# Weight-stationary products: the 512-column and 256-column matmuls of a block grouped by width

## The chip, the cores and the metric

The kernel runs on one core of one Trainium2 chip. The metric is the device time in microseconds of one execution; a version's time is the median over its runs. The profile is one execution of the same program, recorded instruction by instruction.

## The reference

A decoder trunk of two residual layers on 256 tokens of width 1024, in float32, and a last RMSNorm. Every layer is half a SwiGLU feed-forward (inner width 2816), a token mixer, and half of a second feed-forward:

```python
def swiglu(h, w_gate, w_up, w_down):
    return (jax.nn.silu(h @ w_gate) * (h @ w_up)) @ w_down

for layer in range(DEPTH):
    x = x + 0.5 * swiglu(rmsnorm(x, norm_ffn1[layer]), ffn1_gate[layer], ffn1_up[layer], ffn1_down[layer])
    h = rmsnorm(x, norm_mix[layer])
    x = x + (even_mixer if layer % 2 == 0 else odd_mixer)(h, ...)
    x = x + 0.5 * swiglu(rmsnorm(x, norm_ffn2[layer]), ffn2_gate[layer], ffn2_up[layer], ffn2_down[layer])
return rmsnorm(x, norm_final)
```

The even mixer is stick-breaking attention (8 heads) beside a causal pooling, the odd mixer is block attention with 16 heads. Both begin with one projection of h (queries, keys, values) and end with one of the mixed result. So nearly all the arithmetic is products of a 256-row activation with large weight matrices.

## The kernel before

**Precision.** TensorE multiplies in float32r. To keep the accuracy, each operand is split in two parts, hi (rounded to float32r) and lo (the rest), and a product is the sum of three: hi·hi, hi·lo, lo·hi. Weights arrive from DRAM in units of 1 MB into `raw` tiles (L56, on SP's queue). ScalarE casts a unit to its hi part `whi` (L73) and VectorE subtracts to get the lo part `wlo` (L74), in two pieces of 1024 columns each. There are three raw buffers and four buffers each for `whi` and `wlo`; `ahead` keeps the split three units in front of their use.

**Three kinds of product.** `proj` (L336) keeps the activation in the array as the stationary operand and streams weight columns, 512 or 256 at a time. `rows` (L360) does that for the down projections and the output projections, always with 512 columns. `proj_W` (L399), the function that is changed, keeps the weights in the array: for one block of 128 output features it has 16 matmuls, two for each of the eight slices k of the model width. The first takes the hi weights of k and streams 512 columns: the 256 tokens of the hi part of the activation and, right behind them in the tile `xhl`, the 256 of its lo part. Its result covers a whole PSUM bank. The second takes the lo weights of k and streams only the 256 hi columns; its result is added to the second half of the same bank. Below, H is a matmul of 512 columns and L one of 256. Every matmul has its own weight load (PEld in the profile). `whole` then adds the two halves of the bank (ScalarE copy at L408, VectorE add at L409).

**Order of a block before.** H and L alternate with k: H0 L0 H1 L1 and so on to H6 L6, then L7 and H7, so that the first and the last matmul of the group cover the whole bank. The weights of a block come from two units of four slices each, or from one unit of eight.

**Where such blocks are.** Each of the four feed-forwards has five chunks of 512 features, each with four gate blocks and four up blocks: 40 blocks, 160 in all. The mixers' queries and keys are 8 blocks in the even layer and 16 in the odd (`qk_half`). That makes 184 blocks of 16 matmuls, 2944 in all.

**What sets the order of the work.** The program is written in order; a recording layer then places the instructions of each engine with its own estimates of durations, so that VectorE's and ScalarE's order between blocks comes from it. `Tasks` inserts small pieces of attention work (riders) between matmuls: `proj_W` calls `tasks.step()` after every eighth matmul. The PSUM accumulators come from a ring of five banks (`acc`), the small work from a ring of three (`tr`).

Of the kernel before, what the change touches and what calls it, by code (L numbers as in the profile page):

```python
# [13 lines left out]
PSUM = bass.MemoryType.PSUM  # L14
# [14 lines left out]


class WeightStream:
    """Weights from DRAM in 1 MB units, each split exactly into a float32r part and a rest."""

    def __init__(self, nc, pool, raw_bufs, split_bufs, load_ahead, split_ahead):
        self.nc, self.pool = nc, pool
# [22 lines left out]
            self.loaded += 1  # L58

    def split_piece(self):  # L60
        """The next piece of the next unit."""
        i = self.split
        if i not in self.parts:
            self.load_to(i + 1)
            self.now = [
                self.pool.tile([P, 2048], F32R, tag=f"w{x}", name=f"w{x}{i}", bufs=self.split_bufs) for x in ("hi", "lo")
            ]
            self.parts[i] = tuple(t.rearrange("p (k f) -> p k f", k=self.src[i][1]) for t in self.now)
            self.at = 0
        hi, lo = self.now  # L70
        raw = self.raw[i]
        r = slice(self.at, self.at + 1024 // self.pieces(i))
        self.nc.scalar.copy(hi[:, r], raw[:, r])  # L73
        self.nc.vector.tensor_sub(lo[:, r], raw[:, r], hi[:, r].bitcast(F32))  # L74
        self.at = r.stop
        if r.stop == 2048:
            self.raw.pop(i)
            self.split += 1
# [13 lines left out]


class Tasks:
    """Work that rides along with the stream of matrix products, a few blocks after its source."""

    def __init__(self):
        self.now = 0
# [18 lines left out]
def trunk_kernel(  # L117
# [24 lines left out]
    mm = nc.tensor.matmul  # L142
    tasks = Tasks()

# [1 line left out]
    ws = WeightStream(nc, wp, raw_bufs=3, split_bufs=4, load_ahead=6, split_ahead=3)  # L146
    plan = {}

# [36 lines left out]
                add_rows(("odd", "o", r), odd_w_o[0], 2 * r)  # L185
        add_ffn(("f2", layer), ffn2_gate[layer], ffn2_up[layer], ffn2_down[layer])

# [1 line left out]
    x = [ap_.tile([P, D], F32, tag=f"x{m}", name=f"x{m}") for m in range(2)]  # L189
    gains = [tp.tile([P, 384], F32, tag="az", name=f"gains{j}", bufs=2) for j in range(2)]  # L190

# [12 lines left out]
    load_gain(1, 16, norm_ffn2)  # L204
    load_gain(1, 32, even_pool_scale)

# [1 line left out]
    nc.scalar.preload_act_table_set("silu_and_others")  # L208
    warm = cp.tile([P, 512], BF16, name="warm")
    nc.vector.memset(warm, 0.0)  # L210

    def warm_up(n):
        """Keeps the tensor engine busy, so that its clock is up, while it has no operands yet."""
        bank = tr_bank()
        for _ in range(n):
            nc.tensor.matmul(bank, warm[:, 0:P], warm, start=True, stop=True)
# [7 lines left out]
    nc.gpsimd.memset(ones, 1.0)  # L224
    neg1 = cp.tile([P, P], F32, name="neg1")
    nc.gpsimd.memset(neg1, -1.0)
    # ntri[s', s] = -1 where s' >= s
    ntri = cp.tile([P, P], F32, name="ntri")
    nc.gpsimd.affine_select(ntri, neg1, pattern=[[-1, P]], compare_op=ALU.is_ge, fill=0.0, base=0, channel_multiplier=1)
    # past[s, t] = 1 where s < t; cap[s, t] = BIG where s < t, else 0; each twice side by side  # L230
    past = cp.tile([P, 2, P], F32, name="past")
    cap = cp.tile([P, 2, P], F32, name="cap")
    nc.gpsimd.memset(past, 1.0)
# [15 lines left out]
            for key, j, c in (("f1", 0, 0), ("mix", 1, 0), ("f2", 1, 16)) for layer in range(2)}  # L249
    turn_gains(0)  # L250

    # bands[g]: (s, t) weights of the window mean minus the token itself; s 0-127 x t 0-255, s 128-255 x t 128-255
    bands = [cp.tile([P, 384], F32, name=f"band{g}") for g in range(4)]
    # dist[t, s] = t - s, BIG where s > t; t 0-127 x s 0-127, t 128-255 x s 0-255
    dist = cp.tile([P, 384], F32, name="dist")
    gfin = cp.tile([P, D], F32, name="gfin")
    wpool = cp.tile([P, 4, P], F32, name="wpool")
# [28 lines left out]

    tasks.add(24, late_constants)

# [1 line left out]
    xhl = ap_.tile([P, KD, 2, T], F32R, tag="xhl", name="xhl")  # L290
    xh, xl = xhl[:, :, 0, :], xhl[:, :, 1, :]

    def norm_half(m, key, st, between=lambda: None, pool_q=(), square_first=False):
        """xT (times the gain) of token tile m as hi and lo parts, and 1/rms per token."""
        sq = tp.tile([P, D], BF16, tag="sq", name=uid("sq"), bufs=1)
        ss = tp.tile([P, 1], F32, tag=f"ss{m}", name=uid("ss"))
        if square_first:
            nc.scalar.activation(sq, x[m], AF.Square, accum_out=ss)
        t = []
        for q in range(2):  # L300
            bank = tr_bank()
            for j in range(4):
                k = 4 * q + j
                nc.tensor.transpose(bank[:, j * P : (j + 1) * P], x[m][:, k * P : (k + 1) * P], ident)  # L304
            t.append(tp.tile([P, 4, P], F32, tag="h", name=uid("xg"), bufs=2))
            nc.vector.tensor_mul(t[q], bank.rearrange("p (k t) -> p k t", k=4),
                                 gcol[key][:, 4 * q : 4 * q + 4, None].to_broadcast([P, 4, P]))
        for q in range(2):
            dst = (slice(None), slice(4 * q, 4 * q + 4), slice(m * P, (m + 1) * P))
            nc.scalar.copy(xh[dst], t[q])  # L310
            (nc.gpsimd if q in pool_q else nc.vector).tensor_sub(xl[dst], t[q], xh[dst].bitcast(F32))
            between()
        if not square_first:
            nc.scalar.activation(sq, x[m], AF.Square, accum_out=ss)
        ms = tp.tile([P, 1], F32, tag=f"ms{m}", name=uid("ms"))
        nc.gpsimd.tensor_scalar(ms, ss, 1.0 / D, EPS, op0=ALU.mult, op1=ALU.add)
        rstd = tp.tile([P, 1], F32, tag=f"rstd{m}", name=uid("rstd"))
        st["last"] = nc.gpsimd.tensor_tensor(rstd, ms, half, op=ALU.pow).ins
        st[m] = rstd
# [2 lines left out]
        return ((lhs_hi, rhs_hi), (lhs_hi, rhs_lo), (lhs_lo, rhs_hi))  # L322

    def proj(units, m, width):
        """PSUM tile of xT(m)^T @ W for a chunk of columns."""
        bank = acc_bank()
        ms = slice(m * P, (m + 1) * P)
        seq = []
        k = 0
        for i in units:  # L330
            hi, lo = ws.get(i)
            for kk in range(hi.shape[1]):
                seq += passes(xh[:, k, ms], xl[:, k, ms], hi[:, kk, :width], lo[:, kk, :width])
                k += 1
        for n, (a, b) in enumerate(seq):
            mm(bank[:, :width], a, b, start=(n == 0), stop=(n == len(seq) - 1))  # L336
            if n % (3072 // width) == 3072 // width - 1:
                tasks.step()
        return bank

    def rows(acc, groups, ah, al, scale, after, ready=None):
        """x += scale[m] * a^T @ W with the rows of W streamed; after(m) when x of m is complete."""
        total = sum(len(g) for g in groups) * 2
        done = {(m, n): 0 for m in range(2) for n in range(2)}
        for gi, group in enumerate(groups):
# [23 lines left out]
                        after(m, n)  # L369

    def first_products(ug, uu):
        """The products of the first chunk, in the order in which their operands arrive."""
        key = ("f1", 0)
        st = states[key]
        with tc.manual_schedule():
            norm_half(0, key, st, ws.split_piece, (1,), True)
            warm_up(3)
            ws.split_to(1)
            g0 = proj(ug, 0, 256)
            ws.split_to(2)  # L380
            norm_half(1, key, st, pool_q=(0, 1))
            u0 = proj(uu, 0, 256)
            ws.split_to(4)
            g1 = proj(ug, 1, 256)
            u1 = proj(uu, 1, 256)
        return [(g0, u0), (g1, u1)]

    def proj_W(units, f):
        """W[:, f]^T @ xT for all tokens: its large part in the first half of a bank, the rest in the second."""
        bank = acc_bank()  # L390
        n = 0
        k = 0
        fs = slice(f * P, (f + 1) * P)
        for i in units:
            hi, lo = ws.get(i)
            for kk in range(hi.shape[1]):
                both = ((hi, bank, xhl[:, k].rearrange("p a t -> p (a t)")), (lo, bank[:, T:], xhl[:, k, 0, :]))
                for w, dst, rhs in both if k < KD - 1 else both[::-1]:
                    mm(dst, w[:, kk, fs], rhs, start=(n == 0), stop=(n == 2 * KD - 1))  # L399
                    n += 1  # L400
                    if n % 8 == 0:
                        tasks.step()
                k += 1
        return bank

    def whole(bank, tag, bufs):
# [5 lines left out]
    def ffn(tag, st, after):  # L412
# [9 lines left out]
            nc.scalar.copy(hh[dst], v)  # L422
            nc.vector.tensor_sub(hl[dst], v, hh[dst].bitcast(F32))

        # the first chunk goes by token tiles, as one of them is complete before the other
        ug, uu = plan[tag, "g", 0], plan[tag, "u", 0]
        banks = first_products(ug, uu) if ug[0] == 0 else None
        ws.ahead(uu[-1])
# [34 lines left out]
        rows(acc, groups, hh, hl, hs, after)  # L463

    def mixer_tiles(n_f):
        """oT hi and lo, qT, kT and two tiles for 512 columns of token-major data, in the places of hT."""
        o = ap_.tile([P, KF, T], F32R, tag="hth", name=uid("o"))
        qk = ap_.tile([P, KF, T], F32, tag="htl", name=uid("qk"))
        tok1 = tp.tile([P, 2, 512], F32, tag="tok1", name=uid("tok1"), bufs=1)
# [2 lines left out]
        return o[:, 0:8, :], o[:, 8:16, :], q, k, (tok0, tok1)  # L472

    def bcast_rstd(st):
        """1/rms of every token on all partitions: [P, T]."""
        bank = tr_bank()
        dg = tp.tile([P, T], F32, tag="hw", name=uid("diag"), bufs=3)
        for m in range(2):
# [11 lines left out]
            nc.vector.scalar_tensor_tensor(dst[:, f0 + j, :], t, scale, rb, op0=ALU.mult, op1=ALU.mult)  # L490

    def pair_out(f, a0, a1, v, fv, oh, ol):
        """oT of two heads from their weights on (s, t), side by side in the columns of the tensor engine."""
        bank = acc_bank()
        for s, cols, start in ((slice(0, T), slice(0, T), True), (slice(T, 384), slice(P, T), False)):
            for j, a in enumerate((a0, a1)):
# [156 lines left out]
        units = [(plan["odd", "o", r], 2 * r) for r in range(4)]  # L653
        rows(acc, [units[0:2], units[2:4]], oh, ol, (1.0, 1.0), after, ready)

# [1 line left out]
    states = {}  # L657
    part = {}

    def finish(m, n):  # L660
        """The final norm of token tile m, after its half n of the columns."""
        r = slice(n * 512, (n + 1) * 512)
        if not part:
            xg = ap_.tile([P, 2, 2 * D], F32, tag="xhl", name=uid("xg"))
# [65 lines left out]
```

## Time and profile before

| | |
|---|---|
| median of 3 runs | 971.42 us (970.12 to 971.45) |
| profiled execution, first to last instruction | 968.9 us |
| PE busy, matmuls | 958.1 us, 99% of the span |
| PEld busy, weight loads beside them | 814.7 us |
| VectorE, ScalarE, GpSimd busy | 642.9, 521.1, 47.0 us |
| from DRAM | 169.63 MB, 176 GB/s over the span |

The profiled execution's own time is known as its span, 968.9 us; the median of the runs is 2.5 us above it; the difference lies outside the recorded span or is scatter between executions. "L399" is line 399 of the kernel before. A row such as "PE MATMUL acc<-xhl,whi 128*128 128x512" is a matmul that writes a tile `acc` from the streamed `xhl` with the weights `whi`, 128 rows by 128 columns of the array, 512 columns streamed. The recorded duration of a matmul holds its way through the array, so neighbours overlap in the record; what a matmul costs in a stream is the distance from its start to the start of the next, called its pitch here.

### The profile page before, as it was taken

How to read it: one execution, taken by the hardware profiler on the slowest of the kernel's cores; microseconds unless marked ns; L12 is line 12 of the kernel's file. 1: busy time of each engine (PE TensorE's matmuls, PEld its weight loads, DVE VectorE, ACT ScalarE, POOL GpSimd, SP SyncE). 2: the span in 40 equal slices, each digit the busy share in tenths (PEclk: the TensorE clock that was granted, in tenths of full speed). 3: DMA queues.
4: the chain of work that ended last, by engine and by line, in shares of the span. 5: the costliest groups of instructions: out<-in, count | busy, mean ns of one | idle time of the engine just before them, and what ended most of it. 6: DMA issues, size and time to landing. Idle time of an engine off the chain costs nothing.

```text
span 968.9 us, 13444 instructions
## 1 busy us (share of the span) xinstructions
PE 958.1 (99%) x5284; PEld 814.7 (84%) x5284; DVE 642.9 (66%) x1019; ACT 521.1 (54%) x891; POOL 47.0 (5%) x94
## 2 busy tenths in 40 slices
PE   8999999999999999999999999999999999999997
PEld 7888888888889888888888888888888798888885
DVE  6877764577566777754677777347887567777533
ACT  6655553375555555543456655336666466655432
POOL 6700000000000000000000000000000010000000
PEclk9999999999999999999999999999999999999999
DMA  8655554563425555545555555555533455555521
GB/s 313 242 176 193 199 202 187 174 214 134 131 88 178 200 198 202 179 174 181 181 204 174 174 179 202 218 183 173 175 131 121 140 175 174 174 179 200 208 108 44
DMA packets 84312, 171.55 MB, mean 177 GB/s; under 512 B 2788, under 2 KB 25880, under 8 KB 84248
## 3 DMA queue, kind: packets, MB, share of 16 engines
q1 hardware_dynamic: 83960, 170.17, 50.8%
q8 instruction: 41, 0.67, 0.3%
q10 hardware_dynamic: 288, 0.52, 0.1%
q14 instruction: 23, 0.19, 0.1%
HBM read 169.63 MB, written 1.05 MB: 176 GB/s over the span
## 4 chain that ended last, share of the span: by engine, by line
PE 97%; DMA 1%; ACT 0%; DVE 0%; SPq 0%; issue 0%; POOLq 0%; POOL 0%; ACTq 0%
PE acc L399 53%; PE acc L360 29%; PE acc L336 9%; PE tr L304 1%; PE acc L498 1%; DMA x<-in_x_dram 1%; PE tr L605 1%; PE tr L629 1%; PE tr L536 0%; PE tr L520 0%; PE tr L481 0%; DVE wlo L74 0%; SPq L56 0%; PE tr L572 0%; ACT whi L73 0%; PE tr L538 0%
## 5 line engine op out<-in xcount | busy, mean ns | idle before, releaser
L399 PE MATMUL acc<-xhl,whi 128*128 128x512 f32 x1472 | 511.3, 399 | 0.0
L74 DVE TENSOR_TENSOR wlo<-raw,whi 128x1024 fp32r<-128x1024 f32 (+1 forms) x324 | 385.6, 1212 | 174.0 <-ACT whi L73 172.4
L73 ACT CAST whi<-raw 128x1024 fp32r<-128x1024 f32 (+1 forms) x324 | 322.2, 1038 | 168.6 <-PE acc L360 87.0
L399 PE MATMUL acc<-xhl,wlo 128*128 128x256 f32 x1472 | 383.4, 281 | 0.0
L399 PEld LDWEIGHTS acc<-xhl,whi 128*128 128x128 f32 x1472 | 265.4, 188 | 51.9 <-issue 1.7
L399 PEld LDWEIGHTS acc<-xhl,wlo 128*128 128x128 f32 x1472 | 278.0, 189 | 16.5
L360 PE MATMUL acc<-whi,htl 128*128 128x512 f32 x352 | 137.3, 390 | 0.0
L360 PE MATMUL acc<-whi,hth 128*128 128x512 f32 x352 | 137.2, 390 | 0.0
L360 PE MATMUL acc<-wlo,hth 128*128 128x512 f32 x352 | 137.0, 389 | 0.0
L336 PE MATMUL acc<-whi,xhl 128*128 128x256 f32 (+1 forms) x416 | 92.5, 312 | 0.6 <-ACT whi L73 0.6
L360 PEld LDWEIGHTS acc<-whi,htl 128*128 128x128 f32 x352 | 66.1, 188 | 13.7
L360 PEld LDWEIGHTS acc<-wlo,hth 128*128 128x128 f32 x352 | 66.1, 188 | 13.7
L360 PEld LDWEIGHTS acc<-whi,hth 128*128 128x128 f32 x352 | 66.1, 188 | 13.3
L408 ACT COPY hw<-acc 128x256 f32<-128x256 f32 x104 | 38.4, 370 | 67.9 <-PE acc L399 67.9
L336 PEld LDWEIGHTS acc<-whi,xhl 128*128 128x128 f32 x416 | 68.6, 190 | 5.7 <-ACT whi L73 1.1
L409 DVE TENSOR_TENSOR hw<-hw,acc 128x256 f32<-128x256 f32 x104 | 43.3, 417 | 33.6 <-ACT hw L408 33.6
L336 PE MATMUL acc<-wlo,xhl 128*128 128x256 f32 (+1 forms) x208 | 64.2, 309 | 1.1 <-DVE wlo L74 1.1
L409 DVE TENSOR_TENSOR sg<-sg,acc 128x256 f32<-128x256 f32 x80 | 33.3, 417 | 40.5 <-ACT sg L408 40.5
L408 ACT COPY sg<-acc 128x256 f32<-128x256 f32 x80 | 29.4, 368 | 45.3 <-PE acc L399 45.3
L458 ACT CAST hth<-hw 128x256 fp32r<-128x256 f32 x80 | 32.5, 406 | 35.2 <-DVE hw L456 35.2
L452 ACT ACTIVATE sg<-sg 128x256 f32<-128x256 f32 x80 | 31.8, 417 | 29.6 <-DVE sg L451 29.6
L360 PE MATMUL acc<-whi,o 128*128 128x512 f32 x128 | 43.6, 404 | 0.0
(121 smaller groups left out, 597.6 us busy)
## 6 DMA issues: line engine op xcount, KB each, us to landing
raw<-in_ffn_down_dram SPq DMA_DIRECT2D x44, 1024.0 KB, 4.9
raw<-in_ffn_gate_dram SPq DMA_DIRECT2D x43, 1024.0 KB, 4.9
raw<-in_ffn_up_dram SPq DMA_DIRECT2D x43, 1024.0 KB, 4.9
raw<-in_odd_w_qkv_dram SPq DMA_DIRECT2D x12, 1024.0 KB, 5.0
raw<-in_even_w_in_dram SPq DMA_DIRECT2D x8, 1024.0 KB, 5.7
raw<-in_even_w_out_dram SPq DMA_DIRECT2D x4, 1024.0 KB, 4.9
raw<-in_odd_w_o_dram SPq DMA_DIRECT2D x4, 1024.0 KB, 4.9
raw<-in_ffn_gate_dram SPq DMA_DIRECT2D x2, 512.0 KB, 6.1
```

The lines of the kernel that those rows point to most:

```text
L73: self.nc.scalar.copy(hi[:, r], raw[:, r])
L74: self.nc.vector.tensor_sub(lo[:, r], raw[:, r], hi[:, r].bitcast(F32))
L304: nc.tensor.transpose(bank[:, j * P : (j + 1) * P], x[m][:, k * P : (k + 1) * P], ident)
L336: mm(bank[:, :width], a, b, start=(n == 0), stop=(n == len(seq) - 1))
L360: mm(acc[m, n], a, b, start=(done[m, n] == 0 and p == 0), stop=(done[m, n] == total - 1 and p == 2))
L399: mm(dst, w[:, kk, fs], rhs, start=(n == 0), stop=(n == 2 * KD - 1))
L408: nc.scalar.copy(t, bank[:, T:])
L409: nc.vector.tensor_add(t, t, bank[:, :T])
L452: nc.scalar.activation(sg[f - 1], sg[f - 1], AF.Silu)
L458: nc.scalar.copy(hh[:, k, :], h)
L498: mm(bank[j * HD : (j + 1) * HD, cols], v[:, 0 if start else 1, hs], a[:, s], start=start, stop=not start)
L605: mm(zs[j][:, cols], q[r, f, qs], k[r, f, ks], start=True, stop=True)
```

## The change

`proj_W` builds the list of its 16 matmuls first. The hi matmuls of k = 0 to 7 stand in a row, and the eight lo matmuls are put in ahead of the last hi one. The order is now H0 to H6, L0 to L7, H7. The matmuls themselves, their operands, the first and the last of the group and the rhythm of `tasks.step()` (after the eighth and the sixteenth) are as before. The two units of a block are both asked for at its start. Comments and docstrings are gone as well, so the lines behind `proj_W` stand five lower: L399 becomes L396, L408 becomes L403 and so on.

```diff
     def proj_W(units, f):
         bank = acc_bank()
-        n = 0
-        k = 0
         fs = slice(f * P, (f + 1) * P)
-        for i in units:
-            hi, lo = ws.get(i)
-            for kk in range(hi.shape[1]):
-                both = ((hi, bank, xhl[:, k].rearrange("p a t -> p (a t)")), (lo, bank[:, T:], xhl[:, k, 0, :]))
-                for w, dst, rhs in both if k < KD - 1 else both[::-1]:
-                    mm(dst, w[:, kk, fs], rhs, start=(n == 0), stop=(n == 2 * KD - 1))
-                    n += 1
-                    if n % 8 == 0:
-                        tasks.step()
-                k += 1
+        parts = [(hi[:, kk, fs], lo[:, kk, fs]) for hi, lo in map(ws.get, units) for kk in range(hi.shape[1])]
+        seq = [(w, bank, xhl[:, k].rearrange("p a t -> p (a t)")) for k, (w, _) in enumerate(parts)]
+        seq[-1:-1] = [(w, bank[:, T:], xhl[:, k, 0, :]) for k, (_, w) in enumerate(parts)]
+        for n, (w, dst, rhs) in enumerate(seq):
+            mm(dst, w, rhs, start=(n == 0), stop=(n == 2 * KD - 1))
+            if n % 8 == 7:
+                tasks.step()
         return bank
```

PE's order in the first feed-forward, chunk 1: the end of its first block `acc_361` and the first matmul of the next block `acc_381`, before. `whi_262`, `wlo_263` are the parts of the first unit, `whi_270`, `wlo_271` those of the second.

```order
L399 MATMUL acc_361<-xhl,whi_262 128x512
L399 MATMUL acc_361<-xhl,wlo_263 128x256
L399 MATMUL acc_361<-xhl,whi_262 128x512
L399 MATMUL acc_361<-xhl,wlo_263 128x256
L399 MATMUL acc_361<-xhl,whi_270 128x512
L399 MATMUL acc_361<-xhl,wlo_271 128x256
L399 MATMUL acc_361<-xhl,whi_270 128x512
L399 MATMUL acc_361<-xhl,wlo_271 128x256
L399 MATMUL acc_361<-xhl,whi_270 128x512
L399 MATMUL acc_361<-xhl,wlo_271 128x256 x2
L399 MATMUL acc_361<-xhl,whi_270 128x512
L399 MATMUL acc_381<-xhl,whi_262 128x512
```

The same block on PE now, from its first matmul, and the beginning of the next:

```order
L396 MATMUL acc_361<-xhl,whi_262 128x512 x4
L396 MATMUL acc_361<-xhl,whi_270 128x512 x3
L396 MATMUL acc_361<-xhl,wlo_263 128x256 x4
L396 MATMUL acc_361<-xhl,wlo_271 128x256 x4
L396 MATMUL acc_361<-xhl,whi_270 128x512
L396 MATMUL acc_381<-xhl,whi_262 128x512 x4
L396 MATMUL acc_381<-xhl,whi_270 128x512 x3
```

Fourteen changes of width in a block have become two. The last wide matmul still stands next to the first wide one of the next block, which writes another bank. The hi part of the second unit is first needed by the fifth matmul, where it was the ninth; the lo part of the first unit is read until the eleventh, where it was the eighth.

ScalarE's order at the turn from chunk 2's up blocks of the first feed-forward to chunk 3's gate blocks, before (`hw` is an up block, `sg` a gate block, `hth` the hi part of the inner activation):

```order
L73 CAST whi_842<-raw_740 128x1024 x2
L408 COPY sg_869<-acc_852 128x256
L458 CAST hth_134<-hw_830 128x256
L408 COPY sg_889<-acc_872 128x256
L452 ACTIVATE sg_869<-sg_869 128x256
```

The same place now:

```order
L73 CAST whi_842<-raw_740 128x1024 x2
L453 CAST hth_134<-hw_830 128x256
L403 COPY sg_869<-acc_852 128x256
L403 COPY sg_889<-acc_872 128x256
L447 ACTIVATE sg_869<-sg_869 128x256
```

The cast of the finished block has moved ahead of the copy of the next one. VectorE and ScalarE have such exchanges of two neighbours in many places of the feed-forwards; the queues of SP and GpSimd are as they were. On PE, apart from the blocks themselves, two groups of three transposes in the odd mixer stand four matmuls later within their block.

## Prediction

> **What bounds the kernel now.** I read the clock of the core first, then the page's busy times, the chain of work that ended last, PE's waits, and last the starts of single matmuls on the timeline.
>
> ```profile
> core 0: 968.9 us, clock 0.998
> PE 958.1 (99%) x5284; PEld 814.7 (84%) x5284; DVE 642.9 (66%) x1019; ACT 521.1 (54%) x891; POOL 47.0 (5%) x94
> PE 97%; DMA 1%; ACT 0%; DVE 0%; SPq 0%; issue 0%; POOLq 0%; POOL 0%; ACTq 0%
> by line: PE acc L399 53.4%; PE acc L360 29.4%; PE acc L336 9.1%; PE tr L304 1.2%; PE acc L498 1.0%; DMA x<-in_x_dram 0.9%; PE tr L605 0.6%; PE tr L629 0.5%; PE tr L536 0.4%; PE tr L520 0.4%; PE tr L481 0.3%; DVE wlo L74 0.3%; SPq L56 0.2%;
> ```
>
> PE is the bound: 97% of the chain, at a clock of 0.998, so a throttle has nothing to do with it. The changed line, L399, is 53.4% of the chain. PE's waits for others, all that the trace has:
>
> ```profile
> PE tr L216 <- DVE warm L210: 1.2, 1, 1.2
> PE acc L336 <- DVE wlo L74: 1.1, 2, 0.8
> PE acc L336 <- ACT whi L73: 0.6, 1, 0.6
> PE tr L629 <- DVE sn L612: 0.4, 2, 0.2
> PE tr L304 <- DMA x<-in_x_dram: 0.3, 1, 0.3
> ```
>
> None is L399's. A block of `proj_W` therefore lasts as long as its 16 matmuls follow each other, and the question is what one costs beside a neighbour of its own width and beside one of the other width. The chain in order of time merges undisturbed stretches and counts them, which gives pitches:
>
> ```profile
> 14.00 8.64 PE acc L336 x72
> 29.15 16.92 PE acc L399 x96
> 46.25 90.44 PE acc L399 x512
> 210.03 12.69 PE acc L399 x72
> 305.27 107.16 PE acc L399 x608
> 412.43 51.69 PE acc L360 x228
> 492.49 107.16 PE acc L399 x608
> 673.02 12.69 PE acc L399 x72
> 794.76 107.16 PE acc L399 x608
> ```
>
> Columns are start, length and count. The stretch at 412.43 is 512-column matmuls only: 51.69/228 = 0.2267 us each. The one at 14.00 is 256-column matmuls only: 8.64/72 = 0.1200 us. The changed function's stretch at 305.27 is 608/16 = 38 blocks in 107.16 us, 2.820 us a block. Eight H and eight L at the pitches of their like would be 8 x (0.2267 + 0.1200) = 2.774 us. So a block now pays 0.046 us, 1.6%, over what its matmuls cost among their like. Where, the starts show (start, duration; "x2" is two matmuls in one row):
>
> ```profile
> 135.81 0.40 PE L399 MATMUL acc<-xhl,whi 128*128 128x512 f32 x1
> 136.05 0.40 PE L399 MATMUL acc<-xhl,wlo 128*128 128x256 f32 x2
> 136.29 0.40 PE L399 MATMUL acc<-xhl,whi 128*128 128x512 f32 x1
> 136.53 0.40 PE L360 MATMUL acc<-whi,hth 128*128 128x512 f32 x1
> 136.76 0.39 PE L360 MATMUL acc<-wlo,hth 128*128 128x512 f32 x1
> 136.99 0.39 PE L360 MATMUL acc<-whi,htl 128*128 128x512 f32 x1
> 137.21 0.39 PE L360 MATMUL acc<-whi,hth 128*128 128x512 f32 x1
> ```
>
> This is the end of a block, running into the down projection. The two L take 0.24 together, 0.12 each. H beside another bank's H takes 0.24, the next 0.23, and from the third on they are at 0.22 to 0.23.
>
> **The change part by part.** No matmul, load or byte is added or taken away. What goes are twelve changes of width per block.
>
> *Price of a change of width.* The block before has seven turns from H to L, seven back, one L to L and one H to H into the next bank. From 2.820 I take 0.12 for L to L and 0.24 for the bank's change: 2.460, or 0.3514 for a pair of turns. Two pitches among their like are 0.3467. A pair of turns costs 0.0047 us extra.
>
> *The block after.* One pair of turns 0.351, seven L to L at 0.120 = 0.840, six H to H at 0.2267 = 1.360, and the bank's change 0.24: 2.791 us, 0.029 less than 2.820.
>
> *How many blocks.* The seven L399 stretches quoted hold 96 + 512 + 72 + 608 + 608 + 72 + 608 = 2576 matmuls, 161 blocks. The other 23 of 184 are cut up by riders, and a run that is cut gains less; I count half of them. 172.5 x 0.029 = 5.0 us.
>
> *Bounds of that price.* From below: if the bank's change was expensive only because of the alternation, the whole 0.046 goes, in all 184 blocks: 8.5 us. From above, how long a run needs to find its pitch:
>
> ```profile
> 200.10 0.40 PE L336 MATMUL acc<-wlo,xhl 128*128 128x512 f32 x1
> 201.71 0.61 PE L336 MATMUL acc<-whi,xhl 128*128 128x512 f32 x2
> ```
>
> These are the third and the tenth wide matmul after a disturbance by transposes: seven pitches in 1.61 us, 0.230 each. If the six H to H of a block stay there, they cost 1.380, the block 2.811, and the gain is 0.009 x 172.5 = 1.6 us. I take the first value, because in the rows from 136.29 on, which leave a `proj_W` block as every run of H will, the pitch is reached after two matmuls.
>
> *Weights.* The hi part of a block's second unit is needed after four matmuls of 0.227 instead of eight at 0.176 on average, 0.5 us sooner. The tightest place is the first block, which starts at 22.5:
>
> ```profile
> 16.73 3.88 ACT L73 CAST whi<-raw 128x1024 fp32r<-128x1024 f32 x4
> L399 PE MATMUL acc<-xhl,whi x1472: 387/398/505, 22.5 to 901.5; 128*128 128x512 f32 x184
> ```
>
> These four casts are both of its units, done at 20.6; the fifth matmul starts at 23.4. The lo parts are needed later than before. Cost nothing; without this cover it would be one cast's length, about 1 us, once. The first unit's lo part is read three matmuls longer in each block. VectorE's wait before L74 is for something else:
>
> ```profile
> DVE wlo L74 <- ACT whi L73: 172.4, 73, 6.3
> ACT whi L73 <- PE acc L399: 35.0, 39, 1.0
> L74 DVE TENSOR_TENSOR wlo<-raw,whi 128x1024 fp32r<-128x1024 f32 (+1 forms) x324 | 385.6, 1212 | 174.0 <-ACT whi L73 172.4
> ```
>
> VectorE waits 172.4 of 174.0 us for the cast, so a `wlo` buffer held longer delays nobody; the cast waits 35.0 us for L399 to be done with a buffer, and the first unit's hi part now comes free after its fourth matmul instead of its seventh, sooner. Zero. If it did cost, the split would come up to 1 us later per chunk, and the splits run units ahead.
>
> *The exchanges on ScalarE and VectorE.* A copy, a cast or a split changes places with its neighbour. The longest of them is a split piece, 1.2 us by the row above. A block takes 2.8 us and there are five banks, so a bank that is emptied 1.2 us late still is free before PE comes back to it; PE never waits for one in the list above. Zero, or some tenths to either side in the mixers; if all that cover was gone, 20 chunks x 1.2 = 24 us.
>
> *Riders.* The first `tasks.step()` of a block now comes after 7 x 0.227 + 0.12 = 1.71 us instead of 1.41. PE's longest wait for such work is 0.2. Zero.
>
> The sum: 968.9 - 5.0 = 963.9 for a profiled span; with the 2.5 us between span and median, 966.4.
>
> **The rivals.**
>
> *A turn costs nothing, H is slow in this function.* H streams `xhl` here, and a weight tile in the stretch at 412.43; the extra 0.046 may belong to that operand. Then an H among H in `proj_W` costs (2.820 - 0.96)/8 = 0.2325, grouped or not, and the time stays at 971.4. For it speaks the only place where two H of L399 meet, 136.29 to 136.53 above, 0.24; against it that this is a change of banks too, and that the pace inside alternating blocks is not fixed:
>
> ```profile
> 225.36 0.39 PE L399 MATMUL acc<-xhl,whi 128*128 128x512 f32 x1
> 227.10 0.39 PE L399 MATMUL acc<-xhl,whi 128*128 128x512 f32 x1
> ```
>
> Five pairs lie between these two, 0.348 each: the same operands can run at nearly the sum of the undisturbed pitches. [...] Chance 0.11.
>
> *Runs of seven are too short.* The bound from above: 0.230 to the end of the run, a gain of 1.6 us, 969.8. Chance 0.09.
>
> *Slower: the weight load is exposed in the run of L.* Each load needs time under the matmul ahead of it.
>
> ```profile
> L399 PEld LDWEIGHTS acc<-xhl,wlo 128*128 128x128 f32 x1472 | 278.0, 189 | 16.5
> L336 PEld LDWEIGHTS acc<-whi,xhl 128*128 128x128 f32 x416 | 68.6, 190 | 5.7 <-ACT whi L73 1.1 <-issue 1.0
> ```
>
> A load is recorded with 189 ns. Now at least every second matmul is a wide one that covers it with 227; in a run of eight L there is only 120. If the pitch rose to 189, seven L to L in 184 blocks would add 7 x 0.069 x 184 = 89 us, and with the gain of 5 the time would be 1055. The point from which it decides is 0.029/7 = 4 ns: an L pitch above 124 ns makes the kernel slower. Against it stands L336, which has one such load of 190 ns for each of its matmuls and yet runs at 0.1200, 72 in a row. [...] Chance 0.04.
>
> *The exchanges reach PE.* A few late banks or splits, some tenths of a microsecond each in 20 chunks, up to 976. Chance 0.02.
>
> That the change does not do what it says is excluded by the order shown: the runs stand there on PE.
>
> **How the numbers follow.** Forecast 966.4, chance 0.74, its own range 962.9 (8.5 us gained) to 968.5 (a gain of 2.9, between the two values for the run). Adding the rival of short runs at 969.8 leaves 0.17 outside, so the range is 962.9 to 970.5. A measurement of this kernel can tell about 0.2%, 1.9 us, from no change. Faster by more than that: 0.74 and a little of the short runs, 0.75. Within it: most of the rivals at 971.4 and 969.8, 0.19. Slower: 0.06.
>
> **What would show it.** In the profile after: undisturbed stretches of the changed line in the chain with 608 matmuls in 106.1 us instead of 107.16, 2.791 us a block; pitches of 0.227 between the second and the sixth H, and 0.120 between L; PE's waits without an entry of the changed line. Wrong would be an H pitch inside the run of 0.230 or more (no gain), an L pitch above 0.124 (slower), or new waits of the changed line for L73, L74 or the bank's copy.

## The result, and the profile after

The changed kernel takes 965.99 us (median of 4 runs, 965.59 to 966.96) beside 970.96 us for the kernel before on the same chip (4 runs): a ratio of 0.995, 95% interval 0.9936 to 0.9964, 5.0 us faster. Its profiled span is 963.9 us, also 5.0 under the span before.

The clock, the chain by engine and all of PE's waits in the kernel after (in the waits: total us, times, longest):

```profile
core 0: 963.9 us, clock 0.997
PE 99%; ACT 0%; DVE 0%; POOLq 0%; issue 0%; POOL 0%; ACTq 0%
PE tr L216 <- DVE warm L210: 1.2, 1, 1.2
PE acc L336 <- DVE wlo L74: 1.2, 2, 0.7
PE acc L336 <- ACT whi L73: 0.6, 1, 0.6
```

The clock is practically the same (0.997 beside 0.998), PE is 99% of the chain, and the changed line, now L396, has no entry among the waits. So the time should have gone out of the matmuls' pitch. The undisturbed stretches of the chain (start, length, count):

```profile
45.59 89.59 PE acc L396 x512
303.60 106.16 PE acc L396 x608
409.75 51.70 PE acc L360 x228
```

The 608 matmuls, 38 blocks, took 107.16 us before and take 106.16: 2.794 us a block instead of 2.820, 0.026 less. In 184 blocks that would be 4.8 us. Added up over the trace from start to start, the 2944 matmuls of the line, with what waits stand among them, take 523.6 us before and 518.4 after, 5.2 less. The 168 blocks that no rider cuts gained 4.4 us, 0.026 each. The 16 cut ones gained 0.7, and 0.46 of it lies in two blocks of the odd mixer, where the transposes that moved by four matmuls had waited for VectorE before, and wait no longer:

```profile
710.81 0.55 PE L629 MATMUL tr<-ident,p 128*128 128x128 f32 x3 [0.17 <-DVE sn L612]
728.73 0.55 PE L629 MATMUL tr<-ident,p 128*128 128x128 f32 x3 [0.24 <-DVE sn L612]
```

```profile
707.37 0.55 PE L624 MATMUL tr<-ident,p 128*128 128x128 f32 x3
724.96 0.55 PE L624 MATMUL tr<-ident,p 128*128 128x128 f32 x3
```

So about 0.4 us of the gain comes from these two waits and the rest of the line's 5.2 from the pitch. The ends of the span nearly even out: the first block starts 0.45 us earlier (22.63 and 22.18 in the chain), and what follows PE's last matmul is 0.6 longer (7.1 and 7.7). The wide matmuls of L360, which were not touched, still take 51.70/228 = 0.2267 each. Runs of one kind on the timeline; the start of the next run is the end of the one before:

```profile
76.13 2.00 PE L396 MATMUL acc<-xhl,whi 128*128 128x512 f32 x8
77.97 1.12 PE L396 MATMUL acc<-xhl,wlo 128*128 128x256 f32 x8
78.92 2.00 PE L396 MATMUL acc<-xhl,whi 128*128 128x512 f32 x8
...
78.92 0.40 PE L396 MATMUL acc<-xhl,whi 128*128 128x512 f32 x1
79.15 0.40 PE L396 MATMUL acc<-xhl,whi 128*128 128x512 f32 x1
79.39 0.39 PE L396 MATMUL acc<-xhl,whi 128*128 128x512 f32 x1
79.62 0.40 PE L396 MATMUL acc<-xhl,whi 128*128 128x512 f32 x1
79.85 0.39 PE L396 MATMUL acc<-xhl,whi 128*128 128x512 f32 x1
80.08 0.39 PE L396 MATMUL acc<-xhl,whi 128*128 128x512 f32 x1
80.31 0.39 PE L396 MATMUL acc<-xhl,whi 128*128 128x512 f32 x1
80.53 0.39 PE L396 MATMUL acc<-xhl,whi 128*128 128x512 f32 x1
```

Eight H take 1.84 us, 0.027 over 8 x 0.2267. Eight L take 0.95, 0.01 under 8 x 0.120. The single starts in the lower rows show where the 0.027 lies: the first pitches behind the L are 0.23 and 0.24, the last ones 0.22 and 0.23. In the trace's nanoseconds the run reads 233, 236, 228, 233, 231, 226, 227, 227, and the run of L 113, 119 and six times 120. So a block of after still has 0.020 over 2.774, and it sits behind the change from narrow to wide, not evenly over the run.

One row must be read with care. The groups of the changed line, before and after (busy us, mean ns of one):

```profile
L399 PE MATMUL acc<-xhl,whi 128*128 128x512 f32 x1472 | 511.3, 399 | 0.0
L399 PE MATMUL acc<-xhl,wlo 128*128 128x256 f32 x1472 | 383.4, 281 | 0.0
```

```profile
L396 PE MATMUL acc<-xhl,whi 128*128 128x512 f32 x1472 | 372.7, 393 | 0.0
L396 PE MATMUL acc<-xhl,wlo 128*128 128x256 f32 x1472 | 209.7, 284 | 0.0
```

Their busy time falls by 312 us for a gain of 5. A matmul's record overlaps its neighbours', and a group counts overlapping time within itself once: in the alternation every record stands alone in its group, in a run they merge. The counts are equal and the means differ by at most 6 ns; the time of such a stream is read from the pitch.

### The profile page after: what moved, and what is told of

It reads as the page before. It is cut to its first block, busy times and chain, and to the rows that moved or that the text cites. A ratio compares the mean times of both kernels' runs of the same rounds, so it can differ in the third digit from the quotient of the medians.

```text
span 963.9 us, 13433 instructions
## 1 busy us (share of the span) xinstructions
PE 953.1 (99%) x5284; PEld 816.3 (85%) x5284; DVE 645.3 (67%) x1019; ACT 523.8 (54%) x891; POOL 47.4 (5%) x94
## 4 chain that ended last, share of the span: by engine, by line
PE 99%; ACT 0%; DVE 0%; POOLq 0%; issue 0%; POOL 0%; ACTq 0%
PE acc L396 54%; PE acc L360 30%; PE acc L336 9%; PE tr L304 1%; PE acc L493 1%; PE tr L600 1%; PE tr L624 1%; PE tr L531 0%; PE tr L515 0%; PE tr L216 0%; PE tr L476 0%; PE tr L567 0%; PE tr L533 0%; PE tr L532 0%; PE tr L414 0%; DVE wlo L74 0%
## 5 line engine op out<-in xcount | busy, mean ns | idle before, releaser
L74 DVE TENSOR_TENSOR wlo<-raw,whi 128x1024 fp32r<-128x1024 f32 (+1 forms) x324 | 384.3, 1214 | 164.8 <-ACT whi L73 131.5
L396 PE MATMUL acc<-xhl,whi 128*128 128x512 f32 x1472 | 372.7, 393 | 0.0
L396 PEld LDWEIGHTS acc<-xhl,whi 128*128 128x128 f32 x1472 | 264.8, 189 | 47.3 <-issue 0.3
L396 PEld LDWEIGHTS acc<-xhl,wlo 128*128 128x128 f32 x1472 | 200.8, 190 | 15.4 <-issue 1.3
L396 PE MATMUL acc<-xhl,wlo 128*128 128x256 f32 x1472 | 209.7, 284 | 0.0
L360 PE MATMUL acc<-whi,htl 128*128 128x512 f32 x352 | 137.4, 390 | 0.0
L360 PE MATMUL acc<-whi,hth 128*128 128x512 f32 x352 | 137.4, 390 | 0.0
L360 PE MATMUL acc<-wlo,hth 128*128 128x512 f32 x352 | 137.1, 390 | 0.0
L360 PEld LDWEIGHTS acc<-wlo,hth 128*128 128x128 f32 x352 | 66.1, 188 | 13.7
L360 PEld LDWEIGHTS acc<-whi,htl 128*128 128x128 f32 x352 | 66.1, 188 | 13.6
L360 PEld LDWEIGHTS acc<-whi,hth 128*128 128x128 f32 x352 | 66.1, 188 | 13.3
L403 ACT COPY sg<-acc 128x256 f32<-128x256 f32 x80 | 29.5, 369 | 62.0 <-PE acc L396 62.0
L403 ACT COPY hw<-acc 128x256 f32<-128x256 f32 x104 | 38.4, 369 | 42.7 <-PE acc L396 42.1
L454 DVE TENSOR_TENSOR htl<-hw,hth 128x256 fp32r<-128x256 f32 x80 | 33.9, 423 | 18.9 <-ACT hth L453 18.9
```

The source lines that it names most:

```text
L360: mm(acc[m, n], a, b, start=(done[m, n] == 0 and p == 0), stop=(done[m, n] == total - 1 and p == 2))
L396: mm(dst, w, rhs, start=(n == 0), stop=(n == 2 * KD - 1))
L403: nc.scalar.copy(t, bank[:, T:])
L454: nc.vector.tensor_sub(hl[:, k, :], h, hh[:, k, :].bitcast(F32))
```

## The experiments

The theory going in was that a change of width between neighbouring matmuls costs time and nothing else in the change does. The rivals were other things that the new order altered as well: neighbours no longer stream the same columns of `xhl`, hi and lo weight tiles no longer alternate, and the prediction itself had put part of a block's extra on the change of banks. Diffs are against the kernel after, within `proj_W`; `his` and `los` are its lists of the eight wide and the eight narrow matmuls by slice. A block's time is the 38-block stretch of the chain divided by 38; the floor without any extra is 8 x (0.2267 + 0.1200) = 2.774.

### Widths still alternate, but neighbours stream different columns

```diff
+        los = los[4:] + los[:4]
+        seq = [t for k in range(KD - 1) for t in (his[k], los[k])] + [los[7], his[7]]
```

> Wide and narrow matmuls alternate as before, but the narrow one beside the wide one of slice k belongs to slice k+4, so that no two neighbours stream the same columns. Theory (the changes of width cost): 14 changes a block as before, about 2.820 us a block, 971.0 us in all, like before. Rival (the cost came from streaming the same columns of xhl twice in a row): the gain of the change is there as well, about 2.79 us a block, 966.

```profile
306.40 107.16 PE acc L398 x608
```

To the hundredth of a microsecond the stretch of the kernel before; 971.18 us, ratio to before 1.0002 (0.999 to 1.0015). Streaming the same columns twice in a row costs nothing.

### No change of width, but operands alternate

```diff
+        for k, (hi, lo) in enumerate(parts):
+            seq += [(hi, bank[:, :T], xhl[:, k, 0, :]), (lo, bank[:, T:], xhl[:, k, 0, :]), (hi, bank[:, T:], xhl[:, k, 1, :])]
```

> Every wide matmul is cut into two narrow ones (hi tokens, then lo tokens, each with its own weight load), order by slice as before: 24 matmuls of 256 columns a block, hi and lo weights and operands still alternate, no change of width. Theory: 24 x 0.1200 = 2.880 us a block, 184 x 0.060 = 11 us over before, 982. Rival (the alternation of weight tiles or of operands costs, not the width): the 0.046 stays on top, 2.926 a block, 990.

```profile
309.26 109.43 PE acc L397 x912
```

109.43/912 = 0.1200 a matmul, 2.880 a block; 982.5 us (one run). Hi and lo weights, two halves of a bank and two parts of the activation alternate here all the time, with a load for each matmul, and the pitch is that of an undisturbed run. The stretch of L360 shows the same for wide matmuls: hi and lo operands alternate there, at 0.2267 each. What is left of the differences between before and after is the width.

### Groups of two

```diff
+        seq = [t for k in (0, 2, 4) for t in his[k : k + 2] + los[k : k + 2]] + [his[6], los[6], los[7], his[7]]
```

> Groups of two: H H L L, eight changes of width a block instead of 14 (before) and 2 (after). If each change of width has a fixed price, half of the gain: 2.807 us a block, 968.5 us. If instead a wide matmul needs several of its like ahead of it until its pitch settles (after has 233, 236, 228, 232, 231, 227 ns for the first six from the turn on), a group of two never gets there: 233 + 236 + 113 + 119 = 701 ns for four matmuls against 705 in the alternation, 2.806 at best and 2.82 at worst, 968.5 to 971. The pitches in the trace tell.

```profile
305.13 106.89 PE acc L397 x608
```

2.813 a block; 970.25 us, ratio 0.9988 (0.9975 to 1.0002). Of the 14 changes of width six are gone, and with them only 0.007 of the 0.026. A fixed price for a change does not fit, a pitch that needs a run to settle does.

### Groups of four

```diff
+        seq = his[:4] + los[:4] + his[4:7] + los[4:] + his[7:]
```

> Groups of four: H0 to H3, L0 to L3, H4 to H6, L4 to L7, H7; four changes of width a block, two of them from L to H. Theory (behind an L to H change the wide pitches are 233, 236, 228, 232, 231 ns and then 227, and the first narrow pitch is 113; a run that ends sooner pays only its part): 1160 + 697 for the eight wide and 2 x 472 for the eight narrow, 2.801 us a block, 967.6 us. Rival (an L to H change costs 20 ns whatever the run behind it): 2.774 + 0.040 = 2.814, 969.9.

```profile
303.77 106.29 PE acc L397 x608
```

2.797 a block, nearer to the theory's 2.801 than to the rival's 2.814; 966.36 us, ratio 0.9958 (0.9944 to 0.9971). The fixed price has failed here too. The theory's size is not exact either: the wide pitches behind a short run of L are not always the same sequence.

### Every second block reversed

```diff
+        turn[0] = not turn[0]
+        seq = his + los if turn[0] else los + his
```

> Every second block has its order reversed: eight H then eight L, and the next block eight L then eight H. Blocks meet with equal widths, so there is one change of width a block instead of two, and an L to H change only in every second block; the number of bank changes is as before. Theory (what is left over in a block of after, 2.794 against 2.774, is the unsettled pitch behind the L to H change): half of 0.020 goes, 2.784 a block, 964.2 us, 1.8 under after. Rival (the left-over is the change of banks between two wide matmuls, as the prediction had it with 0.24): the changes of banks stay, only half a pair of turns goes, 0.0024 x 184 = 0.4 us, 965.6.

The stretch and the runs of this kernel:

```profile
303.41 105.81 PE acc L400 x608
```

```profile
53.21 2.08 PE L400 MATMUL acc<-xhl,wlo 128*128 128x256 f32 x16
55.12 3.82 PE L400 MATMUL acc<-xhl,whi 128*128 128x512 f32 x16
58.77 2.08 PE L400 MATMUL acc<-xhl,wlo 128*128 128x256 f32 x16
```

2.784 a block, the theory's number; 964.35 us, ratio to before 0.9932 (0.9914 to 0.995). Sixteen H cross from one bank into the next and take 3.65 us, 0.023 over 16 x 0.2267: the same extra as for eight, paid once. In nanoseconds the pitches around the change of banks are 226 and 227. A change of banks between wide matmuls costs nothing here.

### Two blocks at a time, and reversed

Two blocks are issued together into two banks, sixteen H and then sixteen L, the next two the other way round.

```diff
+    def proj_W(units, fs):
+        turn[0] = not turn[0]
+        banks = [acc_bank() for _ in fs]
...
+        seq = his + los if turn[0] else los + his
...
+                if f in (0, 2):
+                    two = proj_W(uu, (f, f + 1))
```

> Two blocks at a time in two banks: sixteen H, then sixteen L, and the next two blocks the other way round, sixteen L then sixteen H. One L to H change in four blocks. Theory (20 ns for each complete L to H change and nothing else): 2.774 + 0.005 = 2.779 us a block, 0.8 us under the reversed single blocks, 963.5 us. Rival (two banks end at nearly the same time, the copy out of them comes late, and PE waits for a bank, as five banks now hold only two and a half pairs): waits of PE for the copy or the add appear, and the time is at or over the 964.3 of the reversed single blocks.

Its stretch, its runs, and all of PE's waits:

```profile
303.07 105.59 PE acc L401 x608
```

```profile
53.17 7.44 PE L401 MATMUL acc<-xhl,whi 128*128 128x512 f32 x32
60.45 4.00 PE L401 MATMUL acc<-xhl,wlo 128*128 128x256 f32 x32
64.28 7.44 PE L401 MATMUL acc<-xhl,whi 128*128 128x512 f32 x32
```

```profile
PE tr L216 <- DVE warm L210: 1.2, 1, 1.2
PE acc L336 <- DVE wlo L74: 1.2, 2, 0.7
PE acc L336 <- ACT whi L73: 0.9, 1, 0.9
PE tr L304 <- DMA x<-in_x_dram: 0.2, 1, 0.2
```

2.779 a block as forecast. Thirty-two H take 7.28 us, 0.03 over 32 x 0.2267, again one payment, and thirty-two L take 3.83. No wait for a bank appears. 962.66 us, ratio to before 0.9918 (0.9905 to 0.9932), whose interval lies below the changed kernel's: this version beats both.

The orders together, from the narrow-to-wide changes that a block has on average:

| order | narrow to wide, per block | block, us | over the floor, ns | for each change, ns |
|---|---|---|---|---|
| alternating (before) | 7 | 2.820 | 46 | 6.6 |
| groups of two | 4 | 2.813 | 39 | 9.8 |
| groups of four | 2 | 2.797 | 23 | 12 |
| grouped (after) | 1 | 2.794 | 20 | 20 |
| reversed in turn | 1/2 | 2.784 | 11 | 21 |
| two blocks, reversed in turn | 1/4 | 2.779 | 5 | 20 |

At 256 columns a complete change costs 20 ns (27 more in the wide run, 7 less at the start of the narrow one), whatever the runs behind it are, once they have eight or more. In shorter runs a change costs less. A run that ends before its pitch has settled would explain that, but the four-group pitches do not follow one sequence, so this part is argued.

### Is it the load under a short matmul?

A narrow matmul's 120 ns are shorter than the 186 to 192 ns of a weight load's record, a wide one's 227 are longer. To see whether that is the cause, the narrow matmul was widened, by streaming a part of the lo tokens as well (a part of lo x lo is added, which the other kernels leave out): first in the alternation. The five kernels of this section have one run each; the uniform stretch of L360 takes 51.69 to 51.73 us in all of them, so their pitches can be compared.

```diff
+        los = [(w, bank[:, 0:448], xhl[:, k].rearrange("p a t -> p (a t)")[:, 0:448]) for k, (_, w) in enumerate(parts)]
+        seq = [t for k in range(KD - 1) for t in (his[k], los[k])] + [los[7], his[7]]
```

> Order as before (wide and narrow alternate), but the narrow matmul streams 448 columns: the 256 hi tokens into the first half of the bank and 192 of the lo tokens behind them, which adds a part of the product lo x lo that before leaves out. By the line through 226.7 ns at 512 and 120.0 at 256 its undisturbed pitch is 200.0 ns, longer than a weight load's 188 to 192; a block without any extra is 8 x 426.7 = 3.413 us. Theory A (any change of width costs, 6.6 ns for each narrow-to-wide change as in before): 3.459 us a block. Theory B (a wide matmul is unsettled only where the matmul ahead of it is shorter than the load that runs under it): 3.413 us a block.

```profile
339.09 133.00 PE acc L397 x608
```

> The same with 384 columns in the narrow matmul: undisturbed pitch 173.3 ns, shorter than the load of 188 to 192; a block without extra is 8 x 400.0 = 3.200 us. Theory A and theory B both 3.246. If both 448 and 384 come out without extra, the limit lies lower than the load's recorded length.

```profile
332.34 125.63 PE acc L397 x608
```

> The same with 320 columns: undisturbed pitch 146.7 ns; a block without extra is 8 x 373.3 = 2.987 us. Theory A and B both 3.033. It places the limit if 384 shows no extra.

```profile
316.90 115.02 PE acc L397 x608
```

3.500, 3.306 and 3.027 us a block: 0.087, 0.106 and 0.040 over the line (1094.76, 1062.38 and 1010.17 us in all). Theory B had no extra at 448 columns, where every load is covered, and the extra is there. Theory A has the right sign, the wrong size in two of three and nearly the right one at 320 columns (0.040 for 0.046), and the line itself, drawn through two widths, was a guess for the others. So the first two were run in the changed order, seven wide, eight narrow, one wide:

> The 448-column kernel in the changed order (seven wide, eight of 448, one wide). In the alternation it took 3.500 us a block, 0.087 over 8 x (226.7 + 200.0), but 200.0 was only a line through two other widths. Theory (the change of width costs, whatever the two widths): a run of 448 has a pitch of about 200 and the block takes 3.413 and some 0.02, 3.43. Rival (448 columns simply take longer, 208 to 211 ns each): 3.48 to 3.50, no gain by the order.

```profile
337.12 131.49 PE acc L397 x608
```

> The 384-column kernel in the changed order; 3.306 us a block in the alternation, 0.106 over the line. Theory: 3.200 and some 0.02, 3.22. Rival (384 columns take 180 ns wherever they stand): 8 x (226.7 + 180) = 3.254 and some 0.02, 3.27.

```profile
328.53 124.13 PE acc L397 x608
```

3.460 and 3.267 us a block (1088.01 and 1052.91 us in all). The order gains 0.040 in both cases (3.500 - 3.460, 3.306 - 3.267), so a matmul that is simply longer, wherever it stands, does not explain the alternation. Neither came to the theory's 3.43 and 3.22; the 448 kernel lies between theory and rival, and the 384 kernel came out at the rival's number, 3.27. Runs of both, 448 first:

```profile
73.47 1.78 PE L397 MATMUL acc<-xhl,wlo 128*128 128x448 f32 x8
75.09 2.00 PE L397 MATMUL acc<-xhl,whi 128*128 128x512 f32 x8
76.93 1.78 PE L397 MATMUL acc<-xhl,wlo 128*128 128x448 f32 x8
```

```profile
70.10 2.01 PE L397 MATMUL acc<-xhl,whi 128*128 128x512 f32 x8
71.95 1.58 PE L397 MATMUL acc<-xhl,wlo 128*128 128x384 f32 x8
73.37 2.01 PE L397 MATMUL acc<-xhl,whi 128*128 128x512 f32 x8
```

Eight of 448 take 1.62 us, 0.2025 each and not 0.200, and the eight wide ones behind them take 1.84, as behind 256. A wide run pays its 0.027 behind a width that is only an eighth narrower, and behind matmuls whose pitch is longer than any load's record, so theory B fails in this order as well. Behind 384 columns it is worse: the eight wide ones take 1.85 us, 0.037 over 8 x 0.2267, with 224 to 236 ns and no settled pitch by the end of the run, and eight of 384 take 1.42 us, 0.177 each and not 0.1733. So the rival's number came with another split, 0.231 and 0.177 instead of 0.227 and 0.180. Why the 384 kernel does not settle stays open.

## Why the prediction was right, point by point

*The bound.* PE's pitch sets the end; no wait of the changed line came. As predicted.

*The block after.* Forecast 2.791, measured 2.794. The sum was right, its split was not. The step "*Price of a change of width*" gave a pair of turns 0.0047 and put the other 0.013 on the change of banks (0.24 for two H). The reversed blocks showed a change of banks free, 16 H with one extra of 0.023, and the table shows a complete narrow-to-wide change at 0.020. The 0.24 was read at the one place of a block before where two H meet, and the first of the two stands directly behind an L, within the unsettled stretch (236 and 233 ns at 136.29 and the start after it, then 227). 0.0047 + 0.013 = 0.018 happens to be about the 0.020 of one complete change, and after has one change and one such place, so the error could not show in its time. It would have shown in a forecast for the reversed order: the rival with the prediction's split said 965.6 there, and 964.35 came, with 2.784 us a block where that split gives 2.792.

*The run of H.* Taken at 0.2267 from the second pitch on; in after it settles with the sixth H behind an L. The rows that the upper bound was read from, 0.230 from the third to the tenth matmul, showed such a settling stretch, and as a mean over eight H, 1.84/8 = 0.230, their number came true. The bound was too high because it put that mean on top of the 0.24 and of the first turn.

*How many blocks.* 172.5 x 0.029 = 5.0 was forecast. The changed line gained 5.2 us: the 168 whole blocks 0.026 each, two cut ones 0.46 together by the waits shown above, and the other 14 cut ones about 0.02 each, so they gained less, but more than the half that was counted. A gain a little too large per block, a count too small and a term that was put at nothing made up for each other; that the sum met the measured 5.0 so closely is luck.

*Weights.* "A `wlo` buffer held longer delays nobody" was wrong by the letter. VectorE now waits for PE to be done with `wlo`:

```profile
DVE wlo L74 <- PE acc L396: 32.6, 39, 1.2
DVE wlo L74 <- ACT whi L73: 131.5, 35, 6.3
ACT whi L73 <- PE acc L396: 20.5, 38, 0.6
```

It took the place of waits for the cast (172.4 before, 131.5 now), and ScalarE's wait for L399's buffers fell from 35.0 to 20.5, as the earlier release of `whi` had it. No entry of PE's waits for either part grew by more than 0.1 us, so the price, zero, held.

*Exchanges and riders.* Zero was forecast for both, from the fact that PE's longest wait for such work was 0.2. The wait it named, "PE tr L629 <- DVE sn L612: 0.4, 2, 0.2", is gone in the list after: the moved transposes gained 0.4 us, so the term was small and not zero. The exchanges show no cost in PE's waits; they were not tried by themselves.

*The rivals.* That H is slow in this function wherever it stands is refuted by the reversed blocks, where a settled H of `proj_W` takes 226 to 227 ns. That runs of seven are too short is half true, as said above; its 969.8 was not. The exposed load is refuted: eight L in 0.95 us, 0.119 each. The Trainium skill, TensorE: Matmul & The Clock Gate, section "The mechanism", lists that weight loads overlap running matmuls only when their row groups differ. The trace does not agree: 32 narrow matmuls, each with a load of 128 rows that is recorded with 186 to 193 ns, follow each other in 3.83 us.

## What to carry to other kernels

In a loop that PE bounds without waits, sum the pitches that long uniform runs of the trace show, and compare them with the pace of the mixed loop: the difference is what the order of the instructions can cost, here 1.6%. Not every width has a uniform pitch even in a run: at 448 columns it went between 199 and 207 ns. Put matmuls of equal width in a row, and let neighbouring groups meet with the same width; of the 46 ns a block that the alternation cost here, groups of two saved 7, groups of eight 26, and two accumulators at a time with the order reversed in turn 41. Look also where small work between the matmuls has moved: two waits gone were 0.4 us here, as much as the new order gains in 15 blocks.

## What the runs showed of the hardware that was not expected

A wide matmul behind a narrower one is slow for five matmuls, not for one: 233, 236, 228, 233, 231 ns and then 227. The narrow run behind a wide one begins 7 ns early instead (113, then 119 and 120). The same 27 ns are paid behind 448 columns as behind 256; behind 384 it is 37 ns, and the pitch has not settled after eight. In short alternations the pitches fall into a repeating pattern whose mean depends on the widths: 6.6 ns for each narrow-to-wide change at 256 columns, and at 384 and 448 columns a block that takes 40 ns more than the grouped one. What in PE makes the pitch settle so slowly stays open; a weight load longer than the matmul beside it, the alternation of operands and the change of banks were excluded, and the trace has no row for what lies between a load and the start of its matmul.
